# When the weight sums for two projections are made: accumulating transfers moved between the stages of a hybrid decoder block

## The chip, the cores and the metric

The kernel runs on one core of a Trainium2 chip. The metric is the device time of one execution in microseconds (us). A core has five engines with instruction streams of their own: PE (TensorE, matrix products; PEld is its weight load), DVE (VectorE), ACT (ScalarE), POOL (GpSimd) and SP (SyncE, which here only issues transfers). A transfer (DMA) is issued by an engine and carried out by the core's 16 DMA engines beside the work of the others.

## The reference

One decoder block on 1024 tokens with a width of 1024, all in float32:

```python
def hybrid_mixer(n, ...):
    z, xBC, dt_raw, q, k, v, r, a1, g_ssd, g_gla = split(n @ w_in)
    y_ssd = ssd_mixer(z, xBC, dt_raw, ...)          # Mamba-2 scan
    y_gla = gla_mixer(q, k, v, r, a1, ...)          # gated linear attention, rmsnorm per head
    merged = sigmoid(g_ssd) * (y_ssd @ w_up_ssd) + sigmoid(g_gla) * (y_gla @ w_up_gla)
    return merged @ w_o

h = x + hybrid_mixer(rmsnorm(x, norm_mix), ...)
h = h + mem_cross_attention(rmsnorm(h, norm_xattn), rmsnorm(mem, norm_mem), w_xq, w_xkv, w_xo)  # q = n @ w_xq
h = h + swiglu(rmsnorm(h, norm_ffn), w_ffn_in, w_ffn_out)
return rmsnorm(h, norm_final)
```

## The kernel before

Every product of two float32 numbers is made of three matmuls: each operand is split into a high part (`whi`, the first of two `ws` or `wd` tiles, made on ACT) and a low part (the rest, made on DVE). Large products use a Strassen-Winograd scheme with seven half-size products named B11, B21, B22, T1, T2, T3, T4 in place of eight. The T's and B22 need sums of quarters of the weight matrix.

The work runs in stages: the memory's keys and values and the norm of x, the input projection in column units (`Unit`, each with seven products; `ru`, `qk`, `gs`, `gg` are lists of such units), and, woven between the units, first the SSD scan (`ssd_steps`) and then the GLA scan (`gla_steps`, eight chunks of 128 tokens). Then come two dense up-projections (`dense(0)` for ys, `dense(1)` for yg, weights `wd` from `Left`), the output projection `wo.steps()`, the query projection `xq.steps()` (both of class `Wide`), the attention, its projection, the feed-forward part and the last norm.

`run(main, (side, rate), ...)` weaves: after each step of `main`, `rate` is added to what is owed, and for each whole one owed a step of `side` is emitted. In the GLA scan the order on the engines comes from a scheduler that follows priorities, and in the SSD scan PE's order is the one written. Transfers marked `pinned` keep their place in the issuing queue.

`Wide` takes its sums of weight quarters ready-made from a DRAM buffer of four blocks, `wos_d` for w_o and `xqs_d` for w_xq. `LEFT` says that T1 reads block 0, T2 block 1, T3 block 2 and B22 block 3; `SEQ` is B11, T1, B22, T2, B21, T3, T4. The loads of a block into a tile `wr` are issued by SP. `weight_sums` fills the blocks with twelve transfers per matrix from DRAM to DRAM, all issued by POOL: four copies of 1 MB into blocks 0, 2, 1 and 3 and eight additions of 512 KB (`accum_op=ALU.add`):

```python
jobs.append([(put(0), q[1, 0], 0), (put(2), q[0, 0], 0), (put(0), q[1, 1], 1), (put(2), q[1, 0], 1),
             (put(1), put(0), 0), (put(3), q[0, 1], 0), (put(1), q[0, 0], 1), (put(3), put(1), 1)])
```

The third number tells whether a job is an addition, and an addition is two transfers. So transfers 1 to 6 make blocks 0 and 2, and the eighth, eleventh and twelfth write block 3.

What else stands on POOL around them: in the scans some additions of the units (`sa`, `raw`: sums of weight quarters), in the GLA scan the power operation on `ss` (in `out`: the reciprocal root mean square of a chunk, by which ACT scales `o` ahead of the transposes of `norm`), in the yg stage the additions `rq<-gates,ga` of `post_yg`, and in the output projection the additions `ssum<-ssum,sq` of the norm's statistics (`Stats`, object `s1`), which `either` deals out to POOL and DVE by a meter of their load. In `norm` the results of a chunk go to DRAM by `yg_d<-qk`, SP's line 1153; `qk<-q_d` (1087) loads a chunk's q, `raw` is a weight load of 1 MB, and `hl<-ys_d` (1396) loads the operands of the first dense stage.

Of the kernel before, what the change touches and what calls it, by code (L numbers as in the profile page):

```python
# [16 lines left out]
P = 128  # L17
# [18 lines left out]
PRIO = 1000  # L36
# [42 lines left out]
def block_kernel(ctx: ExitStack, tc: tile.TileContext, t: dict, out: bass.AP):  # L79
# [3 lines left out]
    DVE, POOL = Meter(nc.vector, now, 0.06, 1.04e-3), Meter(nc.gpsimd, now, 0.08, 2.25e-3)  # L83

    def either(ap, slack=0.0):

        return POOL if POOL.after(ap) - slack < DVE.after(ap) else DVE
# [25 lines left out]
    gg_d = dram("gg_d", D, TOK)  # L113
# [4 lines left out]
    wos_d = dram("wos_d", 2 * D, HALF)  # L118
    xqs_d = dram("xqs_d", 2 * D, HALF)
# [10 lines left out]
    add = lambda e, o, a, b: e.tensor_tensor(o, a, b, ALU.add)  # L130
# [3 lines left out]
    pinned = tc.keep_in_program_order  # L134
# [313 lines left out]
    def run(main, *rest, prio=0):  # L448

        owed = [0.0] * len(rest)  # L450
        for _ in main:
            for i, (g, rate) in enumerate(rest):
                owed[i] += rate
                while owed[i] >= 1.0:
                    owed[i] -= 1.0
                    with tc.high_priority(offset=prio):
                        next(g, None)

    def chain(gs):
        for g in gs:  # L460
            yield from g
# [5 lines left out]
    def singles(units, B, then=()):  # L467

        for u, nxt in zip(units, list(units[1:]) + [None]):
            yield from group([u], B, [nxt] if nxt else then)  # L470
# [11 lines left out]
    def weight_sums(todo):  # L482


        jobs = []
        for A, d, n, k0 in todo:
            put = lambda m, d=d, n=n, k0=k0, kn=A.shape[2]: (
                d[(m * n + k0) * P:(m * n + k0 + kn) * P].rearrange("(k p) c -> p k c", p=P))
            q = {(i, j): A[j][:, :, half(i)] for i in range(2) for j in range(2)}
            jobs.append([(put(0), q[1, 0], 0), (put(2), q[0, 0], 0), (put(0), q[1, 1], 1), (put(2), q[1, 0], 1),  # L490
                         (put(1), put(0), 0), (put(3), q[0, 1], 0), (put(1), q[0, 0], 1), (put(3), put(1), 1)])
        for step in zip(*jobs):
            for o, a, more in step:
                kn = o.shape[1]
                for c in (slice(0, kn // 2), slice(kn // 2, kn)) if more and kn > 3 else (slice(0, kn),):
                    if more:
                        pinned(POOL.dma_start(o[:, c], a[:, c], accum_op=ALU.add))
                    else:
                        pinned(POOL.dma_start(o, a))
                    yield  # L500
# [5 lines left out]
    class Stats:  # L506
        def __init__(s, pl, tag="sq", bufs=1):
            s.pl, s.tag, s.bufs = pl, tag, bufs
            s.sum = pl.tile([P, TOK], F32, name="ssum", tag="ssum", bufs=1)
            s.r = cp.tile([P, NCH], F32, name="rstd", tag="rstd", bufs=2)  # L510
            s.n, s.rest = [0, 0], None

        def take(s, j, ap, cs=ALL, last=False):
            dst = s.sum[:, half(j)][:, cs]
            if s.n[j] == 0:
                ACT.activation(dst, ap, AF.Square)
            else:
                q = s.pl.tile([P, HALF], F32, name="sq", tag=s.tag, bufs=s.bufs)[:, cs]
                ACT.activation(q, ap, AF.Square)
                if last:  # L520
                    s.rest = q
                else:
                    add(either(q), dst, dst, q)
            s.n[j] += 1

        def close(s, j, cs=range(4)):
# [46 lines left out]
    for k in range(NB):  # L573
        p = bank()
# [79 lines left out]
    B = Operands(hb, 4)  # L654
# [234 lines left out]
    ru = w_in_units(R0, 4, store_rows(sr_d))  # L889
    qk = w_in_units(Q0, 2, store_rows(q_d)) + w_in_units(K0, 2, store_rows(k_d))  # L890
    gs = w_in_units(GS0, 4, store_rows(gs_d))
    gg = w_in_units(GG0, 4, store_rows(gg_d))
# [14 lines left out]
    class SSD:  # L907
# [69 lines left out]
        def gate(s):  # L977
            s.y = sp_.tile([P, 4, CH], F32, name="y", tag="y", bufs=3)
            for k in range(4):
                DVE.scalar_tensor_tensor(s.y[:, k], s.L[:, k], dcol[:, s.g * 4 + k:s.g * 4 + k + 1],  # L980
                                         s.py[:, k * P:(k + 1) * P], ALU.mult, ALU.add)
            mul(POOL, s.y, s.y, s.L[:, 4:8])
# [23 lines left out]
    def ssd_steps():  # L1006
        n = len(it)
        it[1].load()
        it[1].load_cs()
        for _ in range(1):  # L1010
            yield
        it[0].lay()
        yield
        it[0].decay()
        for _ in range(7):
            yield
        for i in range(n + 2):
            y, z, a, b, c = (it[k] if 0 <= k < n else None for k in range(i - 2, i + 3))
            if a:
                a.scan()  # L1020
            if z:
                z.sum()
            if y:
                y.norm()
            yield
            if c:
                c.load()
            if b:
                b.lay()
            if a:  # L1030
                a.gate()
            yield
            if z:
                z.stat()
            if b:
                b.decay()
            if c:
                c.load_cs()
            if a:
                a.update()  # L1040
            for _ in range(3 if i == 0 else 1):
                yield
            if a:
                a.square()
                yield
# [14 lines left out]
    st2.close()  # L1060
    sp_ = pool("ssd", 1, stack=st3)
    ssd = ssd_steps()
    with tc.manual_schedule(engines={mybir.EngineType.PE}):
        run(singles(ru + qk + gs[:2], B, gs[2:3]), (ssd, 80 / 70), prio=PRIO)
    drain(ssd)
    st3.close()

# [117 lines left out]
                c.load()  # L1185
            yield

    def dense_sums(w, d):
        return weight_sums([(t[w].rearrange("(j k p) c -> j p k c", j=2, p=P), d, 4, 0)])

    gla = gla_steps()
    wsums = dense_sums("w_o", wos_d)
    run(singles(gs[2:] + gg[:3], B, gg[3:]), (gla, 8 * 5 / 30), (wsums, 0.37), prio=PRIO)
    drain(gla)
    drain(wsums)
    st4.close()
# [6 lines left out]
    ysg_d = dram("ysg_d", D, TOK)  # L1203
# [9 lines left out]
    def quad(src, base, i, j):  # L1213
        q = rp.tile([P, HALF], F32, name="ga", tag="ga")
        SP.dma_start(q, src[base + i * P:base + (i + 1) * P, half(j)])
        return q
# [152 lines left out]
    def dense(no, ins, post, pre=lambda o, j: None, js=JS, left=left):  # L1369

        todo = [(o, j) for o in range(NB) for j in (js if o + 1 < NB else js[::-1])]
        got = [pre(*x) for x in todo[:2]]
        for n, (o, j) in enumerate(todo):
            w = left[NB * no + o]
            if n + 2 < len(todo):
                got.append(pre(*todo[n + 2]))
            cur = got[n]
            p = acc()
            m = 0
            for k in range(NB):  # L1380
                for a, b in ((0, 0), (0, 1), (1, 0)):
                    PE.matmul(p, w[:, a, k], ins[k][:, b, half(j)], start=m == 0, stop=m == 3 * NB - 1)
                    m += 1
            with ahead():
                post(o, j, p, cur)
            yield

    EVEN, ODD = ("op",) * 8, ("op",) * 6 + ("aux",) * 2
    i_ys, i_yg, i_q, i_xo = (paired(x) for x in (EVEN, ODD, EVEN, EVEN))
# [36 lines left out]
    settle_all()  # L1426
    sums["m"] = pool("sa2", 2, stack=st5)
    s1 = Stats(rp, "ga", 6)

    def quad_of(src):  # L1430
        return lambda o, j: quad(src, o * P, 0, j)
# [41 lines left out]
    wo = Wide(t["w_o"], wos_d, post_wo, ("aux",) * 7, ("m", "m", "m", "aux"), xT_d, 0.5)  # L1473

    def wide_side(x, n, m, pin=None):
        for _ in range(n):
            yield
        x.load(1)
        for _ in range(m):
            yield  # L1480
        x.load(2)
        yield
        x.prep(1, pin)
        yield
        x.prep(2, pin)
        yield
# [9 lines left out]
    xq = Wide(t["w_xq"], xqs_d, lambda i, j, u, p: into(i_q, 4 * i + u, j, p, neg=(i, j) == (1, 0)), ("m", "m", "aux", "aux", "m", "aux", "aux"), ("m", "m", "aux"))  # L1496
# [1 line left out]
    def put_xq(o, j, q, g):  # L1498
        ACT.activation(xq.quad(o // 4, j)[:, o % 4], q, AF.Copy, scale=g)

    def waiting(g, n):
        for _ in range(n):
            yield
        for _ in g:
            yield

    run(dense(0, i_ys, post_ys, lambda o, j: gate(gs_d, o, j)), (fetch_gated(yg_d, sr_d, i_yg), 1.0))
    wsums = dense_sums("w_xq", xqs_d)
    run(dense(1, i_yg, post_yg, lambda o, j: (gate(gg_d, o, j), quad(ysg_d, o * P, 0, j))), (wide_side(wo, 8, 4, pinned), 1.0), (wsums, 0.8))
    drain(wsums)  # L1510
    run(wo.steps(), (wide_side(xq, 7, 2), 1.0))


    kv = []
# [127 lines left out]
    for u in range(D_FF // 256):  # L1642
# [5 lines left out]
        gate = Unit(t["w_ffn_in"], 0, 256 * u, post=gpost, key="aux")  # L1648
# [38 lines left out]
    B = Operands(b_xo, 4, order=("B11", "T1", "B21", "B22", "T2", "T3", "T4"))  # L1687
# [219 lines left out]
```

## Time and profile before

| | us |
|---|---|
| median of three runs (1939.82 to 1942.37) | 1939.89 |
| the profiled execution | 1939.03 |
| its span, first to last instruction | 1937.3 |
| PE busy | 1898.9 (98%) |
| DVE, ACT, POOL busy | 1359.5, 882.1, 533.6 |
| mean granted TensorE clock | 0.994 |

All times of rows are microseconds from the span's start. In the rows of a timeline the first number is the start, the second the duration, and the bracket at the end gives the idle time of the engine ahead of it and what ended that idle time. In this execution the SSD scan runs until about 627, the GLA scan until about 803, the ys stage until about 905, the yg stage until about 987, the output projection until about 1063 and the query projection until about 1131.

### The profile page before, as it was taken

The page shows a single profiled execution, that of the slowest core. Times are in us where ns is not written, and L with a number is a line of the kernel's source. Part 1 is how long each engine was busy: PE and PEld are TensorE (multiplying, and loading weights), DVE is VectorE, ACT ScalarE, POOL GpSimd, SP SyncE. Part 2 cuts the span into 40 slices and gives each one's busy share as a digit, 9 for nine tenths or more (in the row PEclk, how much of TensorE's full clock was granted, in tenths as well). Part 3 has the DMA queues.
Part 4 walks back from the last instruction along what each step waited for, and adds up shares of the span by engine and source line. Part 5 has one row for each costly group of instructions (what it writes and reads, how often), then busy time and mean ns, then how long its engine had stood idle before and what let it go on. Part 6 is the DMA issues. An engine that isn't in the chain of part 4 may idle for free.

```text
span 1937.3 us, 26098 instructions
## 1 busy us (share of the span) xinstructions
PE 1898.9 (98%) x9680; PEld 1600.8 (83%) x9680; DVE 1359.5 (70%) x1935; ACT 882.1 (46%) x1521; POOL 533.6 (28%) x426
## 2 busy tenths in 40 slices
PE   7999999999999999899999999999999999999998
PEld 7998787888888888788888888888888888888888
DVE  7765879877776665552288685687878877866566
ACT  7534564555553444652236564553333333345243
POOL 0012324345443322001322100016544534330002
PEclk9999999999999999899999999999999999999999
DMA  9433383456653966984874420424675557397463
GB/s 343 145 94 102 126 303 117 146 164 183 185 163 121 271 193 182 338 288 161 227 202 159 170 85 12 156 94 130 181 194 147 147 166 182 101 298 264 159 222 121
DMA packets 242915, 341.04 MB, mean 176 GB/s; under 512 B 16458, under 2 KB 147764, under 8 KB 242788
## 3 DMA queue, kind: packets, MB, share of 16 engines
q1 hardware_dynamic: 225572, 293.23, 45.0%
q0 software_dynamic: 15488, 39.85, 9.8%
q10 hardware_dynamic: 1728, 6.29, 0.8%
q8 instruction: 76, 1.25, 0.3%
q14 instruction: 51, 0.42, 0.1%
HBM read 249.87 MB, written 129.30 MB: 196 GB/s over the span
## 4 chain that ended last, share of the span: by engine, by line
PE 85%; DVE 7%; DMA 3%; issue 2%; ACT 1%; POOL 1%; SPq 0%; POOLq 0%; DVEq 0%; ACTq 0%
PE acc L51 69%; PE bank L51 14%; DVE cv L73 2%; PE bank L55 2%; DVE wlo L73 2%; DVE o L73 1%; DVE hs L73 1%; DMA yg_d<-qk 1%; DMA hl<-ys_d 0%; DMA qk<-q_d 0%; DMA raw<-in_w_ffn_in_dram 0%; DMA down_d<-in_w_ffn_out_dram 0%; POOL ssum L73 0%; ACT cv L778 0%; DVE gy L73 0%
## 5 line engine op out<-in xcount | busy, mean ns | idle before, releaser
L73 DVE TENSOR_TENSOR wlo<-raw,whi 128x512 fp32r<-128x512 f32 x272 | 243.6, 903 | 97.3 <-ACT whi L233 97.3
L233 ACT ACTIVATE whi<-raw 128x512 fp32r<-128x512 f32 x272 | 169.7, 630 | 253.1 <-PE acc L51 208.8
L51 PE MATMUL acc<-hl,wd 128*128 128x512 f32 x1152 | 266.9, 393 | 6.5 <-ACT wd L233 6.5
L51 PEld LDWEIGHTS acc<-hl,wd 128*128 128x128 f32 x1152 | 217.7, 190 | 54.0 <-ACT wd L233 8.3
L73 DVE TENSOR_TENSOR o<-acc,o 128x512 f32<-128x512 f32 x244 | 166.9, 684 | 82.2 <-PE acc L51 80.5
L51 PE MATMUL acc<-fs 128*128 128x512 f32 (+1 forms) x792 | 155.7, 355 | 0.1
L51 PEld LDWEIGHTS acc<-fs 128*128 128x128 f32 x792 | 130.7, 189 | 20.8 <-issue 0.5
L73 DVE TENSOR_TENSOR fs<-fr,fs 128x1024 fp32r<-128x1024 f32 (+1 forms) x78 | 93.0, 1225 | 36.2 <-ACT fs L233 36.1
L233 ACT ACTIVATE fs<-fr 128x1024 fp32r<-128x1024 f32 (+1 forms) x78 | 74.1, 983 | 94.4 <-PE acc L51 29.2
L73 POOL TENSOR_TENSOR sa<-raw 128x512 f32<-128x512 f32 x42 | 68.3, 1625 | 149.2 <-DMA raw<-in_w_in_dram 80.3
L233 ACT ACTIVATE whi<-sa 128x512 fp32r<-128x512 f32 x96 | 59.7, 626 | 96.1 <-PE acc L51 90.5
L51 PE MATMUL acc<-ws 128*128 128x512 f32 x384 | 88.8, 390 | 0.0
L73 POOL TENSOR_TENSOR raw<-raw,sa 128x512 f32<-128x512 f32 x33 | 44.8, 1357 | 155.7 <-DVE wlo L73 155.7
L51 PEld LDWEIGHTS acc<-ws 128*128 128x128 f32 x384 | 71.9, 188 | 15.2 <-DVE ws L73 0.3
L73 DVE TENSOR_TENSOR wlo<-sa,whi 128x512 fp32r<-128x512 f32 x96 | 72.7, 757 | 8.4 <-ACT whi L233 7.5
L51 PE MATMUL acc<-T4h,whi 128*128 128x512 f32 x192 | 75.9, 395 | 2.6 <-DVE o L73 2.6
L51 PE MATMUL acc<-T3h,whi 128*128 128x512 f32 x192 | 75.7, 394 | 2.0 <-DVE o L73 2.0
L51 PE MATMUL acc<-B22h,wlo 128*128 128x512 f32 x192 | 75.8, 395 | 1.6 <-DVE wlo L73 1.6
L73 POOL TENSOR_TENSOR rstd<-rstd,mhalf 128x4 f32<-128x4 f32 (+1 forms) x7 | 8.7, 1250 | 247.8 <-DVE rstd L73 247.8
L51 PE MATMUL acc<-T1h,whi 128*128 128x512 f32 x192 | 76.3, 397 | 0.0
L51 PE MATMUL acc<-T2h,whi 128*128 128x512 f32 x192 | 75.8, 395 | 0.0
L51 PE MATMUL acc<-B22h,whi 128*128 128x512 f32 x192 | 75.7, 394 | 0.0
(420 smaller groups left out, 5039.2 us busy)
## 6 DMA issues: line engine op xcount, KB each, us to landing
raw<-in_w_in_dram SPq DMA_DIRECT2D x26, 1024.0 KB, 7.8
raw<-in_w_ffn_in_dram SPq DMA_DIRECT2D x22, 1024.0 KB, 6.7
act_d<-o SPq DMA_DIRECT2D x77, 256.0 KB, 3.3
fr<-act_d SPq DMA_DIRECT2D x35, 512.0 KB, 5.6
down_d<-in_w_ffn_out_dram POOLq DMA_DIRECT2D x18, 768.0 KB, 7.3
fr<-down_d SPq DMA_DIRECT2D x20, 512.0 KB, 4.1
ga<-h_d SPq DMA_DIRECT2D x32, 256.0 KB, 6.8
csb<-cs_d SPq DMA_DIRECT2D x15, 512.0 KB, 4.2
```

The lines of the kernel that those rows point to most:

```text
L51: return s.e.matmul(o, x, y, **kw)
L55: return s.e.transpose(o, x, i)
L73: return f(*a, **kw)
L233: pin(ACT.activation(hi, src, AF.Copy))
```

## The change

The first four of the twelve transfers for w_o go out in the SSD scan (`waiting(wsums, 10)` skips ten turns, at a rate of 0.2), and the other eight in the GLA scan at a rate of 0.3 instead of 0.37. The twelve for w_xq leave the yg stage (rate 0.8) and go into the output projection at a rate of 1.0. The additions of `s1` all go to POOL. `waiting` and `dense_sums` move up in the file.

```diff
+    wsums = dense_sums(("w_o", wos_d))
     with tc.manual_schedule(engines={mybir.EngineType.PE}):
-        run(singles(ru + qk + gs[:2], B, gs[2:3]), (ssd, 80 / 70), prio=PRIO)
+        run(singles(ru + qk + gs[:2], B, gs[2:3]), (ssd, 80 / 70), (waiting(wsums, 10), 0.2), prio=PRIO)
...
     gla = gla_steps()
-    wsums = dense_sums("w_o", wos_d)
-    run(singles(gs[2:] + gg[:3], B, gg[3:]), (gla, 8 * 5 / 30), (wsums, 0.37), prio=PRIO)
+    run(singles(gs[2:] + gg[:3], B, gg[3:]), (gla, 8 * 5 / 30), (wsums, 0.3), prio=PRIO)
...
     s1 = Stats(rp, "ga", 6)
+    s1.e = POOL
...
-                    add(either(q), dst, dst, q)
+                    add(s.e or either(q), dst, dst, q)
...
-    wsums = dense_sums("w_xq", xqs_d)
-    run(dense(1, i_yg, post_yg, ...), (wide_side(wo, 8, 4, pinned), 1.0), (wsums, 0.8))
+    run(dense(1, i_yg, post_yg, ...), (wide_side(wo, 8, 4, pinned), 1.0))
+    wsums = dense_sums(("w_xq", xqs_d))
+    run(wo.steps(), (wide_side(xq, 7, 2), 1.0), (wsums, 1.0))
     drain(wsums)
-    run(wo.steps(), (wide_side(xq, 7, 2), 1.0))
```

On POOL, in the GLA scan, before (names are output and inputs, with the shape; `ss` rows are the power operations of successive chunks):

```order
202 L73 TENSOR_TENSOR ss<-ss,mhalf 128x4
203 L73 DMA wos_d<-wos_d 128x4x512
204 L73 DMA wos_d<-in_w_o_dram 128x2x512
205 L73 TENSOR_TENSOR sa<-raw 128x512
206 L73 TENSOR_TENSOR sa<-sa,raw 128x512
207 L73 TENSOR_TENSOR raw<-raw 128x4x128
208 L73 TENSOR_TENSOR ss<-ss,mhalf 128x4
209 L73 DMA wos_d<-in_w_o_dram 128x4x512
210 L73 DMA wos_d<-in_w_o_dram 128x2x512
211 L73 DMA wos_d<-wos_d 128x2x512
212 L73 TENSOR_TENSOR ss<-ss,mhalf 128x4
```

And after:

```order
200 L73 TENSOR_TENSOR raw<-raw 128x4x128
201 L73 TENSOR_TENSOR ss<-ss,mhalf 128x4
202 L73 DMA wos_d<-wos_d 128x4x512
203 L73 DMA wos_d<-in_w_o_dram 128x2x512 x2
204 L73 DMA wos_d<-wos_d 128x2x512
205 L73 TENSOR_TENSOR ss<-ss,mhalf 128x4
206 L73 TENSOR_TENSOR raw<-raw,sa 128x4x128
207 L73 DMA wos_d<-wos_d 128x2x512
```

Four transfers now stand in a row between the power operations of the third and the fourth chunk, where the most between two such operations was three, two chunks before the last.

On SP, at the end of the GLA scan, before:

```order
236 L1396 DMA hl<-ys_d 128x1024
237 L1153 DMA yg_d<-qk 128x8x128
238 L1396 DMA hl<-ys_d 128x1024
239 L1334 DMA raw<-in_w_up_ssd_dram 128x8x256 x2
240 L1396 DMA hl<-ys_d 128x1024 x6
241 L478 DMA gg_d<-o 128x512
242 L1450 DMA whi<-gs_d 128x512
243 L1450 DMA wlo<-gs_d 128x512
244 L1334 DMA raw<-in_w_up_ssd_dram 128x8x256
245 L1153 DMA yg_d<-qk 128x8x128
```

And after:

```order
238 L1403 DMA hl<-ys_d 128x1024
239 L1341 DMA raw<-in_w_up_ssd_dram 128x8x256
240 L1403 DMA hl<-ys_d 128x1024
241 L1341 DMA raw<-in_w_up_ssd_dram 128x8x256
242 L1403 DMA hl<-ys_d 128x1024 x4
243 L1164 DMA yg_d<-qk 128x8x128
244 L1403 DMA hl<-ys_d 128x1024 x2
245 L484 DMA gg_d<-o 128x512
246 L1341 DMA raw<-in_w_up_ssd_dram 128x8x256
```

The last store of the scan now goes out ahead of two hl loads and of the third weight load, and the gates' loads (`whi`, `wlo`) follow it too. Further up, the last chunk's qk loads, which stood right behind a 1 MB load of `raw` (SP's rows 229 to 231 before), now stand ahead of that load (rows 229, 230 and 233), and POOL has no transfer in that part any more. PE's order changes with them: the pieces of the GLA scan come about one product (24 matmuls) earlier between the units' products.

On POOL, in the output projection, before (the yg stage ends with row 242):

```order
239 L73 DMA xqs_d<-xqs_d 128x2x512
240 L73 TENSOR_TENSOR rq<-gates,ga 128x512
241 L73 DMA xqs_d<-xqs_d 128x2x512
242 L73 TENSOR_TENSOR rq<-gates,ga 128x512
243 L73 TENSOR_TENSOR ssum<-ssum,sq 128x512 x9
244 L73 TENSOR_TENSOR rstd<-rstd,mhalf 128x4 x4
```

And after:

```order
229 L73 TENSOR_TENSOR rq<-gates,ga 128x512 x2
230 L73 DMA xqs_d<-in_w_xq_dram 128x4x512 x2
231 L73 DMA xqs_d<-in_w_xq_dram 128x2x512 x4
232 L73 DMA xqs_d<-xqs_d 128x4x512
233 L73 TENSOR_TENSOR ssum<-ssum,sq 128x512 x3
234 L73 DMA xqs_d<-in_w_xq_dram 128x4x512
235 L73 DMA xqs_d<-in_w_xq_dram 128x2x512
236 L73 TENSOR_TENSOR ssum<-ssum,sq 128x512 x3
237 L73 DMA xqs_d<-in_w_xq_dram 128x2x512
238 L73 DMA xqs_d<-xqs_d 128x2x512
239 L73 TENSOR_TENSOR ssum<-ssum,sq 128x512 x4
240 L73 DMA xqs_d<-xqs_d 128x2x512
```

All twelve transfers follow the last `rq` addition, with ten of the fourteen `ssum` additions between them. SP's load of block 3 (B22 of the query projection) waits for the eighth, the eleventh and the twelfth of them, and stands ahead of the load of block 1 (T2). PE's order there stays: the last matmuls of T1, then the first of T2 (four, six before), then B22's 48.

More of the change, by code (lines that the diff above doesn't have):

```diff
@@ L457, in run, with waiting @@
                         next(g, None)
+    def waiting(g, n):
+        for _ in range(n):
+            yield
+        for _ in g:
+            yield
     def chain(gs):
@@ L510, in __init__ @@
             s.r = cp.tile([P, NCH], F32, name="rstd", tag="rstd", bufs=2)
-            s.n, s.rest = [0, 0], None
+            s.n, s.rest, s.e = [0, 0], None, None
         def take(s, j, ap, cs=ALL, last=False):
@@ L1062, in block_kernel, with dense_sums @@
     ssd = ssd_steps()
+    def dense_sums(*todo):
+        return weight_sums([(t[w].rearrange("(j k p) c -> j p k c", j=2, p=P), d, 4, 0) for w, d in todo])
+    wsums = dense_sums(("w_o", wos_d))
     with tc.manual_schedule(engines={mybir.EngineType.PE}):
-        run(singles(ru + qk + gs[:2], B, gs[2:3]), (ssd, 80 / 70), prio=PRIO)
+        run(singles(ru + qk + gs[:2], B, gs[2:3]), (ssd, 80 / 70), (waiting(wsums, 10), 0.2), prio=PRIO)
     drain(ssd)
@@ L1186, in gla_steps @@
             yield
-    def dense_sums(w, d):
-        return weight_sums([(t[w].rearrange("(j k p) c -> j p k c", j=2, p=P), d, 4, 0)])
     gla = gla_steps()
-    wsums = dense_sums("w_o", wos_d)
-    run(singles(gs[2:] + gg[:3], B, gg[3:]), (gla, 8 * 5 / 30), (wsums, 0.37), prio=PRIO)
+    run(singles(gs[2:] + gg[:3], B, gg[3:]), (gla, 8 * 5 / 30), (wsums, 0.3), prio=PRIO)
     drain(gla)
@@ L1499, in put_xq @@
         ACT.activation(xq.quad(o // 4, j)[:, o % 4], q, AF.Copy, scale=g)
[L1501 to L1505, printed above, removed]
     run(dense(0, i_ys, post_ys, lambda o, j: gate(gs_d, o, j)), (fetch_gated(yg_d, sr_d, i_yg), 1.0))
-    wsums = dense_sums("w_xq", xqs_d)
-    run(dense(1, i_yg, post_yg, lambda o, j: (gate(gg_d, o, j), quad(ysg_d, o * P, 0, j))), (wide_side(wo, 8, 4, pinned), 1.0), (wsums, 0.8))
+    run(dense(1, i_yg, post_yg, lambda o, j: (gate(gg_d, o, j), quad(ysg_d, o * P, 0, j))), (wide_side(wo, 8, 4, pinned), 1.0))
+    wsums = dense_sums(("w_xq", xqs_d))
+    run(wo.steps(), (wide_side(xq, 7, 2), 1.0), (wsums, 1.0))
     drain(wsums)
-    run(wo.steps(), (wide_side(xq, 7, 2), 1.0))
     kv = []
```

## The prediction

> **What bounds the kernel now.** I read the busy line of the page first, then the windows for the stages that the change touches, then the chain of waits and the timelines at the places where TensorE pauses.
>
> ```profile
> PE 1898.9 (98%) x9680; PEld 1600.8 (83%) x9680; DVE 1359.5 (70%) x1935; ACT 882.1 (46%) x1521; POOL 533.6 (28%) x426
> 758.00:760.00 2.00, 2.00 (x8) 1.69 (x9) 2.00 (x7) 1.05 (x3) 0.00 (x0) 0.52 0.88 360
> 760.00:762.00 2.00, 2.00 (x14) 2.00 (x13) 1.46 (x3) 0.60 (x1) 0.46 (x1) 0.63 0.67 256
> 800.00:820.00 20.00, 13.97 (x46) 10.42 (x46) 7.72 (x8) 10.88 (x15) 0.00 (x0) 0.74 1.03 375
> 806.00:816.00 10.00, 6.91 (x15) 4.96 (x16) 2.45 (x2) 4.26 (x6) 0.00 (x0) 0.50 1.04 381
> 1000.00:1040.00 40.00, 40.00 (x178) 32.87 (x177) 33.21 (x37) 17.38 (x23) 2.59 (x2) 1.00 0.40 129
> 1040.00:1080.00 40.00, 40.00 (x178) 33.14 (x177) 36.32 (x35) 29.16 (x41) 13.99 (x7) 1.00 0.56 199
> ```
>
> TensorE is the bound: 98% busy over the span. The six window rows give the stretch, its length, the busy time of PE, PEld, DVE, ACT and POOL, then the granted clock, the DMA share and GB/s. So a moved transfer saves time only where TensorE waits now, and costs time only where it makes TensorE wait. Two waits lie beside the transfers that move. The first is near 757 us:
>
> ```profile
> 739.15 0.37 SPq L1153 DMA_DIRECT2D yg_d<-qk  x1
> 741.41 0.39 SPq L299 DMA_DIRECT2D raw<-in_w_in_dram  x1
> 742.10 1.73 SPq L1087 DMA_DIRECT2D qk<-q_d  x1
> 757.89 0.61 PE L51 MATMUL acc<-T3h,whi 128*128 128x512 f32 x1 [1.98 <-DVE o L73]
> ```
>
> The chunk's q load is issued right behind a 1 MB weight load; VectorE runs late on it, and TensorE waits 1.98 us. By the two windows above it then runs at clock 0.52 and 0.63 for 2 us each, a loss of 0.96 + 0.74 = 1.7 us. I call this stall A: 3.7 us. The second opens the dense stage:
>
> ```profile
> 798.99 10.98 DMA yg_d<-qk
> 805.65 1.04 ACT L233 ACTIVATE wd<-raw 128x1024 fp32r<-128x1024 f32 x1
> 806.74 2.07 PE L51 MATMUL acc<-hl,wd 128*128 128x512 f32 x4 [3.68 <-ACT wd L233]
> 810.05 1.06 ACT L233 ACTIVATE wd<-raw 128x1024 fp32r<-128x1024 f32 x1 [3.36 <-DMA yg_d<-qk]
> 811.16 0.80 PE L51 MATMUL acc<-hl,wd 128*128 128x512 f32 x1 [2.35 <-ACT wd L233]
> ```
>
> The last GLA store takes 10.98 us (the DMA share there is 1.03), the second weight split waits for it, and TensorE waits 3.68 + 2.35 us. From 806 to 816 the clock is 0.50, half of 6.91 busy us lost: 3.45. Stall B is 9.5 us. In the output projection (the 1000 and 1040 rows) TensorE is full at clock 1.00, with VectorE at 33 and 36 of 40 us: no wait to win there.
>
> **Trainium skill, clock.** "TensorE: Matmul & The Clock Gate", Part 1, puts the half clock behind at least one idle window of about 3.4 us. Here 1.98 us of idle was followed by 0.52, so the measurement decides; by the page stall A would be 2.0 us, and that term of the sum 1.7 us smaller.
>
> **The change, part by part.**
>
> *Four w_o transfers move into the SSD scan.* POOL's own issue is about a microsecond, and its gaps there hold it:
>
> ```profile
> 573.53 0.56 POOL L73 TENSOR_TENSOR rs<-rs,mhalf 128x1 f32<-128x1 f32 x1 [3.89 <-DVE rs L73]
> 595.22 1.29 POOL L73 TENSOR_TENSOR y<-y,xz 128x512 f32<-128x512 f32 x1 [2.26 <-DVE y L73]
> ```
>
> The transfers are spread over some 50 us, POOL has waited for work at both places, and two raw operations go from VectorE to POOL's place or back without a wait of TensorE beside them. Cost between 0 and 4 us (each issue fully exposed, a microsecond apiece); I take 0, since the idle before these rows is 2 to 4 us.
>
> *Stalls A and B.* The w_o transfers are through some 10 us before (term C below puts the eleventh at 718.1, one more follows), and in SP's order the q and k loads now stand ahead of the 1 MB load: stall A's cause is gone. Bounds 0 to 3.7 us gained; I take 3.7. For B, the store now stands ahead of two hl loads (512 KB each) and a 1 MB weight load that stood in front of it: 2 MB at the 375 GB/s of the 800 row is 5.6 us less of its 10.98. TensorE's order brings the last norm about one product (24 matmuls, 5.4 us at the 40 us for 178 of the 1000 row) earlier too. So it lands about when T4 ends (803.06, by the wait of 3.68 before 806.74), and both splits come in time. Bounds 4.5 (the landing alone) to 9.5 gained; I take 8.5, nearer the upper row because two causes of lateness go.
>
> *POOL as an issuer.* What the rest costs hangs on one thing: while one accumulating transfer is under way, POOL does not get the next one out.
>
> ```profile
> 739.09 1.17 POOL L73 DMA_DIRECT2D wos_d<-in_w_o_dram  x1 [5.89 <-DMA wos_d<-wos_d]
> 755.89 0.84 POOL L73 DMA_DIRECT2D wos_d<-in_w_o_dram  x1
> 761.54 1.16 POOL L73 DMA_DIRECT2D wos_d<-in_w_o_dram  x1 [4.81 <-issue]
> 912.81 0.80 POOL L73 DMA_DIRECT2D xqs_d<-in_w_xq_dram  x1
> 919.80 0.76 POOL L73 DMA_DIRECT2D xqs_d<-in_w_xq_dram  x1 [1.50 <-issue]
> 926.98 1.18 POOL L73 DMA_DIRECT2D xqs_d<-in_w_xq_dram  x1 [3.23 <-issue]
> 936.37 1.18 POOL L73 DMA_DIRECT2D xqs_d<-in_w_xq_dram  x1 [6.88 <-issue]
> 996.14 1.17 POOL L73 DMA_DIRECT2D xqs_d<-xqs_d  x1 [7.02 <-issue]
> DMA to landing us min/median/max: 5.6/6.9/9.2
> ```
>
> Idle before a transfer ended by "issue" is POOL held by the earlier one: 5.65 us from 755.89 to 761.54, 9.4 from 926.98 to 936.37, and 6.7 before 739.09 (idle 5.89 behind an issue of 0.84). The first and the last of the twelve w_xq transfers are 83.3 us apart, eleven gaps of 7.57. The last row is the landing time of these twelve.
>
> *Four w_o transfers in a row in the GLA scan (term C).* In the new order of POOL four stand between two of the small power operations on ss, whose result scales o before TensorE's transposes:
>
> ```profile
> 695.23 1.01 POOL L73 TENSOR_TENSOR ss<-ss,mhalf 128x4 f32<-128x4 f32 x1 [16.24 <-DVE ss L73]
> 713.42 1.03 POOL L73 TENSOR_TENSOR ss<-ss,mhalf 128x4 f32<-128x4 f32 x1 [16.02 <-DVE ss L73]
> 714.49 1.57 ACT L1142 ACTIVATE o<-bank,ss 128x256 f32<-128x256 f32 x4 [1.44 <-POOL ss L73]
> 718.09 0.27 PE L55 MATMUL bank<-ident,o 128*128 128x128 f32 x1
> ```
>
> In the times of before: the first goes out at 696.2, the second 6.7 later, the third and fourth 7.57 apart, the last at 718.1; with 1.2 of its own the power operation starts at 719.3 instead of 713.42, 5.9 late. The slack from scale (ends 716.06) to transposes is 2.0. TensorE waits 3.9 us, and loses 1.7 to a low clock as in stall A: 5.6. With gaps of 5.65 it is 0, with the longest (6.7, 9.4, 9.4) 9.2. I take 5.6, as the w_xq mean is the largest sample of such gaps.
>
> *The w_xq sums in the output projection (term D).* All twelve now begin behind POOL's last rq addition, about 993.4 (in before it ran at 996.90, 3.5 later, behind a held transfer). The stage's second half then needs them:
>
> ```profile
> 996.90 1.74 POOL L73 TENSOR_TENSOR rq<-gates,ga 128x512 f32<-128x512 f32 x1
> 1070.23 0.97 SPq L1252 DMA_DIRECT2D wr<-xqs_d  x2
> 1075.85 1.06 ACT L233 ACTIVATE ws<-wr 128x1024 fp32r<-128x1024 f32 x1 [4.23 <-DMA wr<-xqs_d]
> 1082.85 1.22 DVE L73 SCALAR_TENSOR_TENSOR ws<-rq,ws 128x1024 fp32r<-128x1024 f32 x1
> 1084.88 1.52 PE L51 MATMUL acc<-ws 128*128 128x512 f32 x6
> ```
>
> The load of 1070.23 reads block 3 of xqs_d, which the eighth, eleventh and twelfth transfer write; it landed 5.4 us on. Behind it ACT and VectorE split B22's and then T2's operands without a pause to 1084.07, and TensorE takes T2's at 1084.88, ahead of B22's 48 matmuls: a slack of 0.8. With before's gaps the twelfth goes out at 993.4 + 83.3 = 1076.7, lands at 1083.6 (6.9), the load at 1089.0, the split starts at 1089.2 instead of 1075.85: 13.4 late, 12.6 of it TensorE's. With 1.7 of low clock (B's 3.45 lay behind two waits) D is 14.2. It is 0 if the mean gap is 6.4 or less (twelfth by 1064.1), as in the shortest w_o gap of 5.65; with 8.3 a gap it is 22. I take 14.2, since these are the same transfers, with a DMA share now 0.40 to 0.56 plus their own.
>
> *The rest.* Fourteen ssum additions on POOL instead of nine relieve VectorE of five short ones, hidden under TensorE's 40 of 40. In the yg stage the missing transfers free nothing that TensorE waits for. Bounds −1 to +1; I take 0.
>
> Sum against the profiled execution's 1939.03: −3.7 − 8.5 + 5.6 + 14.2 = +7.6, 1946.6. That execution lies 0.86 under the median of 1939.89, so I forecast 1947.5.
>
> **Trainium skill, transfers.** "DMA: Bandwidth & Descriptors", Anatomy of one DMA — SWDGE (gpsimd) path, fits 2.0 us plus bytes over 436e3: about 4.4 us for 1 MB and 3.2 for 512 KB, an estimate by that page. With it C and D would be 0, and the time that of the first rival. The rows here show 5.6 to 9.2.
>
> **Rivals.**
> 1. *The transfers go through fast.* When the gaps are under 6.4, and C's near 5.65, C and D vanish: 1939.89 − 12.2 = 1927.7. For it: the 5.65 row, and less traffic beside them. Against it: eleven gaps averaging 7.57 in the yg stage. This is the other side, faster; one price decides it, the mean gap. Without D the sum is 1933.3 in medians, so D turns the sign from 6.6 us on, a mean gap of about 6.9.
> 2. *In between.* Gaps from 6.4 to 6.9, C mostly paid, D 0 to 6: 1933 to 1939, say 1936.
> 3. *Stall B stays.* The store still meets full queues (share 1.03) when it is issued earlier, so that only a microsecond is won: 1947.5 + 7.5 = 1955.0. For it: 5 MB of loads are issued around it. Against it: 2 MB now stand behind it in place of ahead.
> 4. *The change doesn't do what it says*, the old order in effect: excluded by the orders, as POOL's rows differ; no chance given.
>
> **How the numbers follow.** The forecast (A and B gone, C and D paid) gets 0.54, rival 1 0.13, rival 2 0.19, rival 3 0.14. The forecast's own range is 1940 to 1953, D from 7 to 20. The whole range, 1930 to 1955, leaves out most of rival 1 and the tail of 3. A measurement tells about 0.2% from no change, 3.9 us: faster is under 1936.0, slower over 1943.8. Faster: 0.13 + 0.10 of rival 2 + 0.04 of the forecast's low tail + 0.02 of rival 3 where D falls away = 0.29. Same: 0.09 of rival 2 + 0.05 of the forecast = 0.14. Slower: the other 0.57.
>
> **What would show it.** Right: no idle of TensorE beside the qk loads near 755 and less than 1 us before the first hl,wd matmuls; POOL's ss operation of the fourth chunk behind three gaps, with a wait of TensorE on ACT's or VectorE's o; twelve xqs_d rows from about 980 on at 7 to 8 us, the load of xqs_d waiting for the last, and TensorE idle over 8 us before acc<-ws of T2, at a low clock afterwards. Wrong: gaps of 6 us in the output projection, or an ss operation not delayed; or a T2 operand that comes by another way.

## The result: 1956.8 us, slower than before and than forecast

The changed kernel takes 1956.8 us (median, 1954.58 to 1958.0) where the kernel before takes 1939.86: a ratio of 1.009, with a 95% interval from 1.0077 to 1.0102. The forecast was 1947.5, within 1930 to 1955: the sign was right, the loss is 17 us instead of 7.6, and the time lies 1.8 us above the range. The profiled execution took 1958.0, its span is 1956.3, 19.0 more than before.

First the busy line of the changed kernel's page, then some of TensorE's waits (what waited, for what, us in total, times, longest), in the changed kernel and below that in the kernel before:

```profile
PE 1904.5 (97%) x9680; PEld 1602.9 (82%) x9680; DVE 1343.6 (69%) x1927; ACT 880.9 (45%) x1521; POOL 546.0 (28%) x434
```

```profile
PE bank L55 <- ACT o L1153: 7.5, 3, 6.4
PE acc L51 <- ACT ws L230: 6.3, 1, 6.3
PE acc L51 <- DVE wk L73: 3.5, 1, 3.5
PE acc L51 <- DVE o L73: 2.3, 3, 1.4
PE acc L51 <- ACT wd L233: 1.4, 2, 0.9
```

```profile
PE acc L51 <- ACT wd L233: 6.5, 3, 3.7
PE acc L51 <- DVE o L73: 4.6, 4, 2.0
```

The first three waits (on ACT's o, on ws and on wk) were not there before. The waits on wd and on VectorE's o, to which stalls B and A belong, are down from 6.5 to 1.4 and from 4.6 to 2.3. To see where the time goes I compare when TensorE has done the same sum of matmul work in the two traces (each matmul counted at its steady duration, 0.227 us for 512 columns). Times of before on the left:

| place (time of before) | changed kernel late by, us | what lies ahead of it |
|---|---|---|
| 500 | 0.4 | |
| 600 | 4.0 | one wait in the SSD scan, where four transfers now stand |
| 700 | 7.3 | first chunks of the GLA scan |
| 740 | 16.7 | four transfers in a row |
| 800 | 12.7 | stall A gone |
| 820 to 1000 | 4.7 | stall B gone |
| 1060 | 9.9 | a weight load late in the output projection |
| 1100 to the end | 19.1 | the load of block 3 |

**The SSD scan.** The meter counts transfers as load of POOL. With the first w_o transfer at 570.43, one raw operation of a unit, on POOL at 578.87 before, went to VectorE, ahead of its `y`. VectorE and TensorE there in the timeline, before and then changed, and two windows of the changed kernel:

```profile
578.64 1.12 DVE L73 SCALAR_TENSOR_TENSOR y<-xz,dcol,bank 128x128 f32<-128x128 f32 x4
579.86 0.63 PE L55 MATMUL bank<-ident,xz 128*128 128x128 f32 x4 [0.18 <-PE bank L55]
```

```profile
580.68 0.69 DVE L73 TENSOR_TENSOR raw<-raw,sa 128x512 f32<-128x512 f32 x1
581.29 1.12 DVE L73 SCALAR_TENSOR_TENSOR y<-xz,dcol,bank 128x128 f32<-128x128 f32 x4
582.50 0.63 PE L55 MATMUL bank<-ident,xz 128*128 128x128 f32 x4 [2.01 <-issue]
582.50:585.00 2.50, 2.50 (x10) 2.07 (x11) 2.50 (x5) 0.63 (x1) 1.48 (x2) 0.71 1.07 398
585.00:587.00 2.00, 2.00 (x6) 1.57 (x5) 1.35 (x2) 1.12 (x4) 2.00 (x2) 0.51 0.51 151
```

In both traces TensorE's transposes start 0.1 us after the end of `y`, which points to a wait for it. TensorE waits 2.01 us instead of 0.18, and the low clock after it (0.71 and 0.51 in the two windows) takes 1.7 more.

**Stalls A and B** are gone. The row of 757.89 has no successor with a wait, and the dense stage opens so, in the timeline and in a window:

```profile
816.59 2.14 PE L51 MATMUL acc<-hl,wd 128*128 128x512 f32 x8 [0.92 <-ACT wd L233]
819.06 11.19 PE L51 MATMUL acc<-hl,wd 128*128 128x512 f32 x48 [0.34 <-DVE wd L73]
```

```profile
800.00:820.00 20.00, 18.74 (x86) 14.88 (x85) 14.64 (x16) 14.98 (x18) 1.01 (x1) 1.00 1.06 385
```

Where TensorE waited 3.68 and 2.35 us it now waits 0.92 and 0.34, at clock 1.00 instead of 0.74, although the DMA share is as high (1.06). The last store was issued at 805.48, ahead of two of the hl loads and the weight load that stood in front of it.

**Term C, four in a row.** POOL, VectorE, ACT and TensorE in the timeline of the GLA scan, then two windows:

```profile
702.17 1.03 POOL L73 TENSOR_TENSOR ss<-ss,mhalf 128x4 f32<-128x4 f32 x1 [4.24 <-DVE ss L73]
703.18 0.82 POOL L73 DMA_DIRECT2D wos_d<-wos_d  x1
708.87 1.16 POOL L73 DMA_DIRECT2D wos_d<-in_w_o_dram  x1 [4.88 <-DMA wos_d<-wos_d]
718.23 1.16 POOL L73 DMA_DIRECT2D wos_d<-in_w_o_dram  x1 [8.20 <-issue]
724.99 1.14 POOL L73 DMA_DIRECT2D wos_d<-wos_d  x1 [5.60 <-issue]
725.70 1.50 POOL L73 TENSOR_TENSOR ss<-ss,mhalf 128x4 f32<-128x4 f32 x1
718.47 0.69 DVE L73 SCALAR_TENSOR_TENSOR qk<-qk,e 128x512 f32<-128x512 f32 x1 [6.85 <-DMA qk<-q_d]
719.08 0.31 DVE L73 TENSOR_SCALAR ss<-ss 128x4 f32<-128x4 f32 x1
727.24 1.57 ACT L1153 ACTIVATE o<-bank,ss 128x256 f32<-128x256 f32 x4 [6.75 <-POOL ss L73]
727.77 2.12 PE L55 MATMUL bank<-ident,o 128*128 128x128 f32 x8 [6.36 <-ACT o L1153]
```

```profile
720.00:730.00 10.00, 3.64 (x17) 2.80 (x16) 4.74 (x15) 3.25 (x8) 2.21 (x2) 0.67 0.95 218
730.00:740.00 10.00, 10.00 (x44) 8.68 (x44) 4.16 (x6) 3.17 (x6) 6.66 (x5) 0.81 0.79 169
```

From the first to the last of the four, 21.8 us pass. The power operation reads what VectorE makes of `ss` at 719.08, behind a wait of 6.85 us for the q of the next chunk. That is done at 719.4, so the power operation starts 6.3 us after its operand. TensorE waits 6.36 us, and the clock of 0.67 and 0.81 takes about 3 more (0.33 of 3.64 and 0.19 of 10): about 9.4, the step from 7.3 to 16.7 in the table.

**Output projection.** In the timeline the first and the last of the w_xq transfers, and what ACT and TensorE wait for; then SP's wait for them (in the list of its waits) and their landing times:

```profile
998.85 0.83 POOL L73 DMA_DIRECT2D xqs_d<-in_w_xq_dram  x1
1050.50 1.06 ACT L233 ACTIVATE ws<-wr 128x1024 fp32r<-128x1024 f32 x1 [5.17 <-DMA wr<-in_w_o_dram]
1060.38 15.48 PE L51 MATMUL acc<-ws 128*128 128x512 f32 x60 [3.46 <-DVE wk L73]
1083.00 1.14 POOL L73 DMA_DIRECT2D xqs_d<-xqs_d  x1
1094.36 1.06 ACT L233 ACTIVATE ws<-wr 128x1024 fp32r<-128x1024 f32 x1 [13.56 <-DMA wr<-xqs_d]
1101.16 0.79 PE L51 MATMUL acc<-ws 128*128 128x512 f32 x1 [6.27 <-ACT ws L230]
```

```profile
SPq L1259 <- DMA xqs_d<-xqs_d: 11.5, 1, 11.5
```

```profile
DMA to landing us min/median/max: 5.4/6.3/9.5
```

The first and the last transfer are 84.2 us apart (83.3 before, in the yg stage). SP's load of block 3 is held 11.5 us for the last of them, and ACT idles 13.56 us on it. But TensorE's wait of 6.27 there is only the second one. At 1060.38 it has already waited 3.46 us on an operand chain that began with a w_o load landing late: issued between 1036.96 and 1037.97, used at 1050.50.

### The profile page after: what moved, and what is told of

The parts are those of the page before. It is cut to its first block, busy times and chain, and to the rows that moved or that the text cites. A ratio compares the mean times of both kernels' runs of the same rounds, so it can differ in the third digit from the quotient of the medians.

```text
span 1956.3 us, 26098 instructions
## 1 busy us (share of the span) xinstructions
PE 1904.5 (97%) x9680; PEld 1602.9 (82%) x9680; DVE 1343.6 (69%) x1927; ACT 880.9 (45%) x1521; POOL 546.0 (28%) x434
## 3 DMA queue, kind: packets, MB, share of 16 engines
q10 hardware_dynamic: 1728, 6.29, 0.8%
## 4 chain that ended last, share of the span: by engine, by line
PE 74%; DVE 8%; issue 7%; DMA 5%; POOL 3%; ACT 2%; SPq 0%; POOLq 0%; DVEq 0%; ACTq 0%
PE acc L51 61%; PE bank L51 12%; DVE cv L73 2%; DVE wlo L73 2%; PE bank L55 2%; DMA raw<-in_w_in_dram 1%; POOL ssum L73 1%; DVE o L73 1%; DMA zr<-sz_d 1%; DVE ws L73 1%; DVE hs L73 1%; DMA hl<-ys_d 0%; POOL sa L73 0%; POOL xqs_d L73 0%; DMA down_d<-in_w_ffn_out_dram 0%
## 5 line engine op out<-in xcount | busy, mean ns | idle before, releaser
L73 DVE TENSOR_TENSOR wlo<-sa,whi 128x512 fp32r<-128x512 f32 x96 | 71.9, 749 | 13.7 <-ACT whi L233 12.7
L51 PE MATMUL acc<-T2h,wlo 128*128 128x512 f32 x192 | 76.0, 396 | 0.0
L51 PE MATMUL acc<-T2l,whi 128*128 128x512 f32 x192 | 75.9, 395 | 0.0
```

The lines of the kernel that those rows point to most:

```text
L51: return s.e.matmul(o, x, y, **kw)
L73: return f(*a, **kw)
```

## Experiments

Each kernel below the first row was run together with the kernel before on the same chip, where the kernel before measured 1938.48 to 1938.55 (medians). "Start" is TensorE's first matmul of the output projection in the profiled execution, "rest" is the span less that time; before has 986.77 and 950.5.

| kernel | median us | ratio to before, 95% interval | start | rest |
|---|---|---|---|---|
| changed | 1956.8 | 1.009 (1.0077 to 1.0102) | 991.48 | 964.8 |
| w_xq sums alone moved | 1950.04 | 1.0056 (1.0038 to 1.0074) | 986.94 | 962.9 |
| w_o sums alone moved | 1941.25 | 1.0008 (0.9996 to 1.0021) | 985.92 | 950.2 |
| before and idle transfers | 1958.23 | 1.0098 (1.0068 to 1.0127) | 986.40 | 969.2 |
| the same, additions on POOL | 1953.11 | 1.0066 (1.0047 to 1.0085) | 985.76 | 964.6 |
| changed, additions as before | 1954.05 | 1.0068 (1.0044 to 1.0092) | 987.93 | 962.9 |
| changed, half the w_xq transfers in yg | 1945.16 | 1.0029 (1.0013 to 1.0046) | 984.84 | 956.6 |
| all w_o transfers in the SSD scan | 1932.69 | 0.9967 (0.9955 to 0.9979) | 976.73 | 950.9 |
| w_o alone, rate 0.37 | 1929.12 | 0.9937 (0.9911 to 0.9962) | 977.15 | 950.3 |
| the same, additions on POOL | 1930.88 | 0.9964 (0.9951 to 0.9977) | 978.16 | 953.9 |
| changed, rate 0.37 | 1944.45 | 1.0035 (1.002 to 1.005) | 975.64 | 966.7 |

**One part at a time.** The w_xq move alone, with everything else of before:

```diff
-    run(dense(1, i_yg, post_yg, ...), (wide_side(wo, 8, 4, pinned), 1.0), (wsums, 0.8))
-    drain(wsums)
-    run(wo.steps(), (wide_side(xq, 7, 2), 1.0))
+    run(dense(1, i_yg, post_yg, ...), (wide_side(wo, 8, 4, pinned), 1.0))
+    wsums = dense_sums("w_xq", xqs_d)
+    run(wo.steps(), (wide_side(xq, 7, 2), 1.0), (wsums, 1.0))
+    drain(wsums)
```

> Only the query projection's sums move into the output projection; the w_o sums and the statistics' additions stay as before. Theory (parts add up): this part alone carries both delays after 1000 us of the changed kernel, 5.3 (a late weight load at about 1055) and 9.3 (the load of block 3): 1939.9 + 14.6 = 1954.5, within 2. Rival (the delays need the late start that the scan's delay gives, or the statistics' additions on POOL): under 1948.

It was 10.9 us slower (0.56%), between the theory and the rival. The loss lies in the rest alone (962.9), but only a part of it came in the way expected. ACT's, VectorE's and TensorE's rows:

```profile
1046.18 1.06 ACT L233 ACTIVATE ws<-wr 128x1024 fp32r<-128x1024 f32 x1 [4.24 <-DMA wr<-in_w_o_dram]
1058.16 0.69 DVE L73 TENSOR_TENSOR ssum<-ssum,sq 128x512 f32<-128x512 f32 x1 [3.99 <-POOL ssum L73]
1060.74 16.20 PE L51 MATMUL acc<-ws 128*128 128x512 f32 x60 [8.36 <-DVE wk L73]
```

The late w_o load is here too: ACT waits 4.24 us for it. Behind it an addition of the statistics on VectorE waits 3.99 us for the one before it on the same tile, which stands on POOL behind a held transfer. TensorE waits 8.36 us for VectorE, for both. After that the data are in time: no wait on block 3 is left. So the load of block 3 costs only what other delays have left of it.

The w_o move alone, against the changed kernel:

```diff
-    s1.e = POOL
...
-    run(dense(1, i_yg, post_yg, ...), (wide_side(wo, 8, 4, pinned), 1.0))
     wsums = dense_sums(("w_xq", xqs_d))
-    run(wo.steps(), (wide_side(xq, 7, 2), 1.0), (wsums, 1.0))
+    run(dense(1, i_yg, post_yg, ...), (wide_side(wo, 8, 4, pinned), 1.0), (wsums, 0.8))
     drain(wsums)
+    run(wo.steps(), (wide_side(xq, 7, 2), 1.0))
```

> Only the w_o sums move (four into the SSD scan, eight at a rate of 0.3 in the GLA scan); the w_xq sums stay in the yg stage. Theory: SSD +4.0, smaller waits to 700 us +3.3, the four in a row +9.5, stalls A and B -3.1 and -8.0, some order effects: the 4.7 us that the changed kernel is late at 820 us, so 1944.6, within 2. Rival (the gains A and B are taken by other waits in the yg stage, where the w_xq sums now stand): over 1950.

Measured 1941.25, by the interval between no change and 4 us slower, and under what was expected. In its profiled execution TensorE was 0.9 us ahead at the start of the output projection, where the changed kernel was 4.7 late. Up to the yg stage the two programs are the same, and in that stage neither gains nor loses on the kernel before. The SSD scan makes most of the difference: at 600 us this kernel was 0.4 late, the changed one 4.0, and the five others with the same scan 0.1 to 3.4. A part is the change's: in all seven TensorE waits 1.61 to 2.53 us at the place near 581, where four executions of before's order (its own and the three kernels that leave the w_o sums as they were) wait 1.07 at most. The rest is the execution's: a low clock followed that wait, for 1.7 us, in the changed kernel and in one other, and in the other five it did not. The two parts together, 10.9 + 1.5 by the ratios, are 4 to 5 short of the 17; what is left falls to the third edit, the statistics (below).

**What of the loss is traffic and what the wait for data.** Twelve more transfers of the same form, into a buffer that nothing reads, beside the kernel before:

```diff
+    idle_d = dram("idle_d", 4 * HALF, HALF)
+    wsums = dense_sums("w_xq", idle_d)
-    run(wo.steps(), (wide_side(xq, 7, 2), 1.0))
+    run(wo.steps(), (wide_side(xq, 7, 2), 1.0), (wsums, 1.0))
+    drain(wsums)
```

> The kernel before, and besides its own w_xq sums in the yg stage twelve more transfers of the same form from w_xq into a buffer that nothing reads, in the output projection: traffic and POOL's time as in the change, no load that waits for them. Theory: the late weight load remains, +5.3, and the wait for block 3 is gone: 1945.2, within 2. Rival 1 (traffic costs nothing, everything is the wait for the data): 1940. Rival 2 (all of it is traffic and POOL being busy): 1954.

Rival 2, and more: 19 us slower, without anyone waiting for the sums.

```profile
1047.33 0.69 DVE L73 TENSOR_TENSOR ssum<-ssum,sq 128x512 f32<-128x512 f32 x1 [13.03 <-POOL ssum L73]
1067.85 15.83 PE L51 MATMUL acc<-ws 128*128 128x512 f32 x60 [16.00 <-DVE wk L73]
```

The first six transfers started at 1003.81, later than in the change, so POOL's first addition came later and VectorE waited 13.03 us behind it, and 6.36 more at the next such place (1065.28). To take these waits away, all additions go to POOL (with the change's `s.e` in `Stats`):

```diff
     s1 = Stats(rp, "ga", 6)
+    s1.e = POOL
```

> As the kernel with twelve idle transfers in the output projection, but all the statistics' additions on POOL. Theory: VectorE's wait of 16 us for POOL's sums vanishes; traffic alone remains, which makes a weight load late by some 5 us: 1944, within 3. Rival (POOL's chain of sums delays TensorE just as well through the norm, or the traffic does it alone): 1953 or more.

The rival again: 1953.11. VectorE's wait is gone, but the waits move to ACT, whose squares share a ring of six buffers with POOL's additions:

```profile
1081.05 0.63 ACT L519 ACTIVATE sq<-wk 128x512 f32<-128x512 f32 x1 [6.98 <-POOL ssum L73]
```

TensorE waits 4.54 us at the place of the late load and 4.2 in two pieces at the place of block 3, although SP's load of it is not held here. So a held POOL reaches TensorE by three ways: through VectorE, through ACT, or through the data.

**The statistics on POOL**, undone in the changed kernel:

```diff
-    s1.e = POOL
```

> The changed kernel with the statistics' additions dealt out by the meter as before. Theory: VectorE's additions then stand behind POOL's on the same tile, and POOL is held by transfers; VectorE waits 8 us or more at about 1055, which takes the place of both delays of the changed kernel: between 1949 and 1957, no wait for block 3. Rival (the additions on POOL are what delays the changed kernel): under 1946.

1954.05, within what was expected. This kernel is the two moves together, and its ratio, 1.0068, is what the two make alone (1.0056 and 1.0008). Its rest is 962.9, that of the w_xq move alone, and 1.9 under the changed kernel's; by the ratios the third edit costs 4.3, with intervals that overlap. The late load stays in both kernels (ACT waits 4.25 us for it here); what the additions on POOL trade is VectorE's wait for POOL against the wait on block 3, and they do not gain.

**A smaller dose.** Six of the twelve w_xq transfers stay in the yg stage:

```diff
+    wsums = dense_sums(("w_xq", xqs_d))
-    run(dense(1, i_yg, post_yg, ...), (wide_side(wo, 8, 4, pinned), 1.0))
+    run(dense(1, i_yg, post_yg, ...), (wide_side(wo, 8, 4, pinned), 1.0), (wsums, 0.4))
-    wsums = dense_sums(("w_xq", xqs_d))
     run(wo.steps(), (wide_side(xq, 7, 2), 1.0), (wsums, 1.0))
```

> The changed kernel with six of the twelve w_xq transfers left in the yg stage (rate 0.4) and the other six in the output projection. Theory: the last goes out some 45 us earlier, at about 1038 of this run, so block 3 is there before its load is issued, and the late weight load falls largely away: 14 under the changed kernel less what is left of traffic, 1942 to 1946. Rival (any transfer in the output projection costs its share): 1950, half way.

1945.16: the last transfer goes out at 1026.56, block 3 is never waited for, and the rest is 956.6, 8.2 under the changed kernel's. Six us more than before's rest stay. Most of that is not the transfers': the kernel with all the statistics' additions on POOL and no transfer there (below) has 953.9. Against that the six cost 2.7 us and the changed kernel's twelve 10.9, so by these profiles the rival, half the price for half the transfers, does not hold.

**Where the row of four comes from.** The w_o move alone, the rate in the GLA scan back at that of before; POOL's order then has at most one transfer between two power operations there:

```diff
-    run(singles(gs[2:] + gg[:3], B, gg[3:]), (gla, 8 * 5 / 30), (wsums, 0.3), prio=PRIO)
+    run(singles(gs[2:] + gg[:3], B, gg[3:]), (gla, 8 * 5 / 30), (wsums, 0.37), prio=PRIO)
```

> As the kernel with only the w_o move, but the eight transfers in the GLA scan at the rate of before, 0.37; in POOL's order at most one then stands between two power operations. Theory: the four in a row cost 8 us there and the stalls A and B stay gone, so about 8 under that kernel: 1933, within 3, TensorE's wait on ACT's o of 5 to 6 us gone. Rival (the wait on o comes from the scan's order or from the first four transfers, not from the row of four): as that kernel, 1941.

1929.12, the fastest kernel here: 0.63% under before (0.38 to 0.89). Its longest waits of TensorE hold no ACT o and no wd any more (0.5 us on wd are left):

```profile
PE acc L51 <- DVE wlo L73: 4.7, 8, 1.7
PE bank L55 <- DMA rows<-in_norm_mix_dram: 2.8, 1, 2.8
PE bank L55 <- issue: 2.5, 1, 2.5
PE acc L51 <- DVE o L73: 2.3, 3, 1.5
```

Four kernels here have the row of four, and in them TensorE waits 6.36, 5.70, 6.96 and 6.29 us on ACT's o at that place. The three at 0.37 and the one with all twelve transfers in the SSD scan have no such wait. Two transfers of the kernel at 0.37 are still issued at 731.85 and 750.13, and both stalls are gone all the same.

The same with the statistics on POOL:

```diff
+    s1.e = POOL
```

> The kernel with only the w_o move at a rate of 0.37 in the GLA scan, with all the statistics' additions on POOL besides. Theory: with no transfers in the output projection they are hidden there, 1929 again, within 2. Rival (VectorE runs slower beside POOL's additions, and the chain of fourteen ends late): 2 to 5 more, 1931 to 1934.

By the medians 1.8 more, by the ratios 5 more with intervals that just overlap, by the profiles 3.7 more in the rest: two waits on VectorE's wk, 0.74 and 1.22 us, are new. That speaks for the rival, and its size stays open between 2 and 5 us.

And the changed kernel with that rate:

```diff
-    ... (gla, 8 * 5 / 30), (wsums, 0.3), prio=PRIO)
+    ... (gla, 8 * 5 / 30), (wsums, 0.37), prio=PRIO)
```

> The changed kernel, only the rate of the eight transfers in the GLA scan back at 0.37. Theory: the row of four and its 9.5 us are gone, the delay of about 14.5 in the output projection stays: 1929 + 14.5 = 1944, within 3, so 11 to 14 under the changed kernel. Rival (TensorE reaching the projections earlier only lengthens its wait for the twelfth transfer): over 1950.

1944.45: the row of four, with what else changes in the order at that rate, cost the changed kernel about 12 us by the medians (11 by the ratios; 14 for the pair without the w_xq move). TensorE now waits 8.09 us at block 3, where the changed kernel waited 6.27, so a little of the gain comes back as a longer wait there (the rest is 966.7 against 964.8).

**All w_o transfers in the SSD scan**, and not counted by the meter, against the w_o move alone:

```diff
-        run(singles(ru + qk + gs[:2], B, gs[2:3]), (ssd, 80 / 70), (waiting(wsums, 10), 0.2), prio=PRIO)
+        run(singles(ru + qk + gs[:2], B, gs[2:3]), (ssd, 80 / 70), (waiting(wsums, 10), 0.33), prio=PRIO)
...
-                        pinned(POOL.dma_start(o[:, c], a[:, c], accum_op=ALU.add))
+                        pinned(POOL.e.dma_start(o[:, c], a[:, c], accum_op=ALU.add))
...
-                        pinned(POOL.dma_start(o, a))
+                        pinned(POOL.e.dma_start(o, a))
```

> All twelve w_o transfers go into the SSD scan, spread over it at a rate of 0.33, and the meter that deals out additions to POOL or DVE does not count transfers; the w_xq sums stay in the yg stage. Theory: stalls A and B vanish as in the change (-3.1, -8.0), the four in a row and the two raw operations that went to DVE are gone: 1939.9 - 11 = 1929, within 3. Rival 1 (each transfer in the SSD scan delays TensorE by about a microsecond through POOL): 1941. Rival 2 (A and B were gained by the order that the eight late transfers bring, not by their absence): 1939 to 1942.

1932.69, 0.7 us above what was expected, and 10 us ahead at the start of the output projection: A and B vanish here too, with no transfer left in the GLA scan, so both rivals fall. The raw operation near 581 is back on POOL (580.70), and TensorE's wait there is 0.73 us, with three times as many transfers in that scan: this speaks for the operation that the meter moved as the cause of the wait, and against the transfers themselves. What A and B share in this kernel, in the changed one and in the one at 0.37 is the new order of the scan's pieces and SP's; whether the order alone would do, with all twelve transfers late, was not tried.

## Why the prediction was right in sign and wrong in size

- **Stalls A and B** (−3.7 and −8.5): right. The table shows −4.0 between 740 and 800 and −8.0 between 800 and 820. All four executions of before's order show both stalls (A 1.98 to 2.31 us), and in the eight kernels with the w_o move A is gone and at most 1.3 us of B's waits are left. But the 1.7 us of low clock that A was priced with were chance: in the three other executions with A the clock stayed at 1.00 after it (last section).
- **Term C** (+5.6): the step that failed first, by its slack. The row went out as forecast, 21.8 us against 21.9, and the power operation was nearly as late as forecast, 6.3 us against 5.9. The wrong number was the slack of 2.0 us from the scale to the transposes. I took it from the rows of before, though the order had changed: VectorE's `ss` now stood behind a late q, and TensorE was out of other work at 721.4. With POOL free the transposes could have started at about 721.0 (1.6 us after the power operation, as in the chunk before: 702.17, 703.24, 703.77), so the slack was about 0.4. The wait was 6.36 instead of 3.9, the low clock took 3 instead of 1.7, and TensorE lost 9.4 instead of 5.6, just over the upper bound of 9.2. In the three other executions with the row the same step is 7 to 9 us.
- **The four in the SSD scan** (0, bound 4): I looked for waits of TensorE beside the two raw operations in the old trace and found none. In the new order TensorE waits for one of them, 1.6 to 2.5 us, and with the low clock the changed kernel lost 4.0. The small waits in the first chunks of the GLA scan, some 3 us, had no term: 0.67 us on ACT's o at 667.37 and 0.47 at 703.77 are part of them.
- **Term D** (+14.2): the mechanism stood, link by link: eleven gaps of 7.65 against 7.57, and ACT's split 18.5 us later than before, 13.8 without the 4.7 that the kernel was late already, against 13.4. Its amount is nearly that of the whole stage, 14.3 in the rest. But it is not one wait, and the idle time over 8 us ahead of T2 that I had named as a sign did not come. 5.2 were lost earlier, to a load that came late beside the traffic, and block 3 added 9.2. As block 3 is what TensorE waits for last, the 5.2 are a part of D and not on top of it. I took the full TensorE of the 1000 and 1040 rows as proof that nothing else there had a limit; the half-dose and the idle transfers show that traffic and the held POOL cost on their own.
- **The rest** (0, −1 to +1): the statistics on POOL cost 2 to 5 us without transfers beside them. I had counted what VectorE is spared and not the longer additions in POOL's chain (1.3 us each and more, on VectorE 0.7); that these are the cause is likely, but not shown.
- The sum was 7.6; C at 9.4, the first chunks at 3 and the SSD scan at 4 bring it to 18.4, most of the profiled 19.0. The range ended at 1955 because its upper end was rival 3, with B unremoved, and held nothing for several bounds reached at once. Rival 1, transfers that go through fast, is refuted by POOL's rows: the mean gap is 7.65 us in the output projection and 7.3 in the row of four, where the rival needed under 6.4. The Trainium skill's fit ("DMA: Bandwidth & Descriptors", Anatomy of one DMA — SWDGE (gpsimd) path) would be 3.2 us for 512 KB and 4.4 for 1 MB, an estimate by that page. The trace does not agree: the landing of the twelve w_xq transfers took 5.4 to 9.5.

## What to carry to other kernels

A transfer that an engine must issue is work on that engine's queue. Here the next one held everything behind it for as long as the last was under way, 7.65 us a transfer on average, so the number in a row between two small operations that others wait for matters as much as the stage. When a change moves the order, take slacks and due times from the new order and only durations from the old trace. A meter that counts the moved transfers moves other work too. And a stage in which TensorE never waits is not a stage with room: ahead of T2's operands there were 0.8 us.

## What the runs showed of the hardware that was not expected

Transfers from DRAM to DRAM on POOL's queue slow the loads on SP's. Landing of the 1 MB load of xT and, median, of the 256 KB stores of h_d in the output projection, before and then changed (us at the end of a row):

```profile
wk<-xT_d SPq DMA_DIRECT2D x1, 1024.0 KB, 8.7
h_d<-wk SPq DMA_DIRECT2D x12, 256.0 KB, 2.2
```

```profile
wk<-xT_d SPq DMA_DIRECT2D x1, 1024.0 KB, 13.5
h_d<-wk SPq DMA_DIRECT2D x11, 256.0 KB, 6.2
```

The other kernels with w_xq transfers in the output projection agree: 12.3 to 14.5 us for xT with twelve of them, 9.5 with six, and 8.7 or 8.8 in two kernels with none.

The other surprise is the clock after a wait of about 2 us. Stall A in the kernel with the w_xq move alone, the same program as before up to there:

```profile
759.09 0.47 PE L51 MATMUL acc<-T3h,whi 128*128 128x512 f32 x1 [2.19 <-DVE o L73]
760.00:762.00 2.00, 2.00 (x20) 2.00 (x19) 2.00 (x7) 1.02 (x3) 0.00 (x0) 1.00 1.04 420
```

TensorE waits longer than in the profile of before (1.98) and goes on at clock 1.00, where that one showed 0.52 and 0.63. I looked at TensorE's waits between 400 and 1300 us of the twelve profiles. Of the eight waits of 1.98 to 2.53 us that do not follow close on another, three were followed by a low clock that took 1.7 us, and five by none; after every wait of 2.67 us or more (to 16.00) the clock fell, for 1.4 to 4.0 us. This makes a part of the spread of one program between executions. The changed kernel, the w_o move alone, the half-dose and the one with the additions as before have the same instructions up to the yg stage, and are 4.7 us late, 0.8 ahead, 1.9 ahead and 1.2 late there. A term of 4 us read from one profile needs a second one.
